# Moving the attention's subtractions and additions from GpSimd to VectorE

## The chip, the core and the metric

The kernel runs on one NeuronCore of a Trainium2 chip. The core has TensorE (PE in the profile), which multiplies matrices and writes to the accumulators in PSUM; VectorE (DVE), ScalarE (ACT) and GpSimd (POOL), which work element by element; and queues that issue transfers. Each engine runs its instructions in the order in which the program issued them to it. The metric is the device time of one execution in microseconds (us), lower is better.

## The reference

Two transformer blocks over a sequence of 1024 tokens of 1024 channels, all in float32. The change touches only the attention of the second block, which has two branches:

```python
def mla_attention(q_nope, q_rope, k_nope, k_rope, v):     # 8 heads, 64 + 32 channels for q and k, 64 for v
    ...
    logits = (einsum(qn, k_nope) + einsum(qr, k_rope)) * B_QK_DIM ** -0.5
    logits = where(causal, logits, NEG_INF)
    return einsum(softmax(logits), v)

def dsa_sparse_attention(q, k, v, iq, ik, iw, positions, rel_table):   # 8 heads, one k and v for all of them
    ...
    _, sel = top_k(score, 256)                            # per query, over the keys up to it
    logits = einsum(q, k[sel]) * A_HEAD_DIM ** -0.5 + bias
    return einsum(softmax(logits), v[sel])
```

Behind it `merged = gate_a * (y_a @ w_branch_a) + gate_b * (y_b @ w_branch_b)`, an output product with a residual, and an MLP.

## The kernel before

To keep float32 accuracy every matrix operand is held as two parts, a high half `hi` (the value rounded as ScalarE writes it) and a low half `lo = raw - hi`; a product is then three matmuls (`mm3`: hi hi, hi lo, lo hi). So nearly every operand needs a copy by ScalarE (the high half) and a subtraction behind it (the low half).

The attention (`attention`) is 16 heads one after the other, first the 8 MLA heads, then the 8 sparse (DSA) heads; a head runs over pairs of 128-row query blocks in the order 3, 0, 2, 1. `front` computes the scores into PSUM (tile `pd`, two buffers), a row maximum on VectorE, and the exponential on ScalarE. `back` transposes the probabilities on TensorE into PSUM (tile `ps`, four buffers), copies the high half (ScalarE) and subtracts for the low half (VectorE, tile `t`), multiplies with the values and scales the output.

Nothing there is issued at once. Every piece is a step of a `Plan`: an engine, an estimated duration, a rank (a wished-for time), the function that issues the instruction, the steps that it needs, and the buffers that it takes and frees. `Plan.run` plays the engines forward with the estimates and always issues what can start first; among steps of an engine that can start within 0.05 us the lowest rank goes first. This writes the order of every engine's queue. Engines named in the steps are `PE`, `ACT`, `DVE` and `Pool`. A transfer (`transfer`) is a step of 1.06 us on `Pool`, which issues it, followed by an estimated landing time. Buffers that the steps take are `pd` (2), `ps` (4), `t2` (8, of 512 columns) and `t4` (2, of 1024 columns).

The steps that the change touches make inputs of the heads and of the stage behind:

- `mla_begin`, line 2684: low half of the rotated keys, in three copies (32 rows of 1024), rank -20 and up.
- `q_rope`, line 2717: the sum of the two rotated terms of the rope queries, 512 columns, four times. Behind it `rope_rows` loads 32 rows for each MLA head (line 2787), copies the high half and subtracts (line 2798).
- `dsa_begin`, line 2904: low half of the sparse branch's keys (64 rows of 1024); `dsa_inputs`, line 2854: the same for the queries of each sparse head, behind a transfer into a `t4` buffer.
- `y_done`, line 2621: low half of y_a after each pair of sparse heads but the last (128 rows of 1024); the last pair's is on VectorE already (line 2623).
- `yb_part`, line 2934: low half of y_b, which was stored to memory and is loaded into `t2` buffers, eight times 512 columns.
- `branch_weights`, line 2472: low half of the first three weight tiles of the branch products (128 rows of 1024). Its engine is the weight stream's `lo_engine`, which line 2459 sets to GpSimd for the time of the plan and line 2465 sets back.

GpSimd's queue also issues the transfers named above. Ahead of the attention, at the end of `z_phase`, nine further weight tiles are split with GpSimd's help (line 2367 sets `lo_engine`); line 2407 sets it to VectorE before the attention starts.

## Time and profile before

| | us |
|---|---|
| median of three timed runs | 2674.82 |
| lowest and highest of them | 2673.29, 2676.94 |
| the profiled execution | 2677.41 |
| its span, first to last instruction | 2675.6 |

The profile is one execution. Its views used here: the page (busy time of each engine over the span), busy time by stretch, groups of instructions, waits (who waited for whom) and the timeline of an engine. Durations of single instructions overlap a little with the next one, so the time that an instruction takes from its engine is read between two starts. All instructions carry line 183, a recording helper, so the groups are told apart by their tiles: `t` are the `t2` and `t4` buffers, `u` the large operand buffers, `ps` and `pd` the accumulators, `wr`, `wh` and `wl` a weight tile as loaded and its two halves, `topk` the buffer that also holds the statistics of the softmax.

### The profile page before, as it was taken

What the parts mean: (1) busy time and instruction counts of PE and PEld (TensorE: products, weight loads), DVE (VectorE), ACT (ScalarE), POOL (GpSimd) and SP (SyncE); (2) the same over time, 40 slices, a digit from 0 to 9 for tenths busy, and PEclk for the clock granted to TensorE, in tenths of its full rate; (3) what the DMA queues carried; (4) which work ended last, traced back from release to release, by engine and by line L of the source; (5) the groups of instructions that cost most, each with busy time, mean ns of one, the idle gap of its engine ahead of it and who ended that gap; (6) DMA issues with size and microseconds to landing.
All of it is one profiled execution on the core that took longest, in us unless ns stands there. A gap on an engine that the chain in (4) does not pass through costs nothing.

```text
span 2675.6 us, 33677 instructions
## 1 busy us (share of the span) xinstructions
PE 2588.6 (97%) x12052; PEld 2079.3 (78%) x12052; DVE 1895.2 (71%) x3239; ACT 1334.5 (50%) x2208; POOL 366.4 (14%) x393
## 2 busy tenths in 40 slices
PE   4999999999999999999999999999999999999998
PEld 4777777777888878777878778777887888887886
DVE  6684576887665466877889878887557566646668
ACT  4562114565444343445676477885135554443334
POOL 5141111100000021000211411420000000002111
PEclk8999999999999999999999999999999999999999
DMA  6536638655445597645545501444455564459784
GB/s 207 186 106 217 192 116 272 220 185 152 147 138 197 188 268 212 190 116 170 138 150 169 185 15 40 145 149 136 149 171 160 185 224 142 154 186 268 189 252 146
DMA packets 371735, 456.98 MB, mean 171 GB/s; under 512 B 34014, under 2 KB 262285, under 8 KB 371053
## 3 DMA queue, kind: packets, MB, share of 16 engines
q1 hardware_dynamic: 332096, 311.07, 37.2%
q0 software_dynamic: 39136, 143.60, 18.8%
q8 instruction: 95, 1.56, 0.2%
q14 instruction: 76, 0.61, 0.1%
q10 hardware_dynamic: 332, 0.14, 0.0%
HBM read 361.70 MB, written 96.18 MB: 171 GB/s over the span
## 4 chain that ended last, share of the span: by engine, by line
PE 73%; DVE 10%; issue 6%; DMA 5%; ACT 4%; POOL 1%; SPq 0%; POOLq 0%; ACTq 0%; DVEq 0%
PE ps L183 50%; PE pd L183 22%; DVE u L183 4%; DVE t L183 3%; ACT u L183 2%; DMA t<-in_w_in 2%; ACT t L183 1%; DVE wl L183 1%; DVE tiny L183 1%; POOL u L183 1%; DMA slabd<-t 1%; DVE topk L183 1%; DMA u<-opd 1%; ACT wh L183 1%; DMA t<-aqd 0%
## 5 line engine op out<-in xcount | busy, mean ns | idle before, releaser
L183 PE MATMUL ps<-u,wh 128*128 128x512 f32 x3696 | 1173.3, 398 | 6.7 <-ACT u L183 4.2
L183 PEld LDWEIGHTS ps<-u,wh 128*128 128x128 f32 x3696 | 690.0, 188 | 177.0 <-ACT u L183 5.7
L183 PE MATMUL ps<-u,wl 128*128 128x512 f32 x1848 | 731.9, 396 | 0.6 <-DVE wl L183 0.6
L183 PE MATMUL pd<-u,wh 128*128 128x512 f32 x1472 | 480.3, 407 | 2.5 <-ACT u L183 1.6
L183 PEld LDWEIGHTS ps<-u,wl 128*128 128x128 f32 x1848 | 347.5, 188 | 86.4 <-DVE wl L183 1.3
L183 DVE TENSOR_TENSOR wl<-wr,wh 128x1024 fp32r<-128x1024 f32 (+3 forms) x213 | 229.9, 1080 | 162.5 <-ACT wh L183 156.0
L183 PEld LDWEIGHTS pd<-u,wh 128*128 128x128 f32 x1472 | 274.1, 190 | 70.9 <-issue 5.7
L183 PE MATMUL pd<-u,wl 128*128 128x512 f32 x736 | 292.4, 397 | 0.0
L183 ACT ACTIVATE wh<-wr 128x1024 fp32r<-128x1024 f32 (+3 forms) x225 | 207.2, 921 | 168.3 <-PE pd L183 78.9
L183 ACT ACTIVATE t<-ps 128x512 f32<-128x512 f32 (+7 forms) x347 | 176.6, 523 | 177.0 <-PE ps L183 164.1
L183 DVE TENSOR_TENSOR t<-ps,t 128x384 fp32r<-128x384 f32 (+3 forms) x354 | 192.5, 563 | 90.6 <-PE ps L183 59.7
L183 ACT ACTIVATE t<-t 128x512 f32<-128x512 f32 (+2 forms) x261 | 162.8, 626 | 168.9 <-DVE t L183 90.5
L183 DVE TENSOR_TENSOR u<-u 128x1024 fp32r<-128x1024 f32 (+3 forms) x154 | 154.1, 1002 | 68.1 <-ACT u L183 62.6
L183 ACT ACTIVATE u<-t 128x512 fp32r<-128x512 f32 (+4 forms) x158 | 127.5, 815 | 136.7 <-DVE t L183 110.8
L183 ACT ACTIVATE wh<-u 128x1024 fp32r<-128x1024 f32 x96 | 101.3, 1055 | 182.8 <-PE ps L183 116.8
L183 DVE TENSOR_TENSOR wl<-u,wh 128x1024 fp32r<-128x1024 f32 x96 | 117.3, 1222 | 88.0 <-ACT wh L183 87.9
L183 PE MATMUL ps<-wh,u 128*128 128x512 f32 (+1 forms) x576 | 173.7, 383 | 0.6 <-DVE u L183 0.6
L183 POOL DMA_DIRECT2D u<-opd x64 | 55.2, 1027 | 862.8 <-DMA u<-opd 758.2
L183 PEld LDWEIGHTS pd<-u,wl 128*128 128x128 f32 x736 | 139.2, 189 | 34.0
L183 PE MATMUL pd<-wh,u 128*128 128x512 f32 x512 | 162.0, 396 | 0.0
L183 ACT ACTIVATE u<-u 128x1024 fp32r<-128x1024 f32 (+8 forms) x111 | 97.6, 889 | 126.1 <-issue 57.1
L183 ACT ACTIVATE u<-ps 128x512 f32<-128x512 f32 (+2 forms) x171 | 95.9, 575 | 115.2 <-PE ps L183 109.2
(191 smaller groups left out, 3507.6 us busy)
## 6 DMA issues: line engine op xcount, KB each, us to landing
wr<-in_w_fc SPq DMA_DIRECT2D x64, 512.0 KB, 4.5
opd<-t SPq DMA_DIRECT2D x128, 256.0 KB, 3.7
u<-opd POOLq DMA_DIRECT2D x64, 512.0 KB, 10.5
wr<-in_w_ff SPq DMA_DIRECT2D x64, 512.0 KB, 4.5
wr<-in_w_in SPq DMA_DIRECT2D x60, 512.0 KB, 3.9
t<-opd SPq DMA_DIRECT2D x48, 512.0 KB, 4.8
u<-in_w_ada POOLq DMA_DIRECT2D x32, 512.0 KB, 4.7
wr<-in_w_out SPq DMA_DIRECT2D x32, 512.0 KB, 3.9
```

What stands on the lines that cost most here:

```text
L183: return fn(*args, **kw)
```

## The change

Each of the steps above that computes on `Pool` names `DVE` instead, with an estimate of 1.14 us (1024 columns) or 0.6 us (512 columns) in place of 2.4 and 1.3, and issues its instruction on `nc.vector`. The line that set the weight stream's engine to GpSimd for the plan is taken out. The transfers keep their engine. Nothing else is changed; the arithmetic is the same.

```diff
--- before.py
+++ after.py
@@ -2456,7 +2456,6 @@
                 t0, t1 = (clock(x + 15 * P) + self.LAG for x in (c0, c))
                 self.back(t0, n, p, (t1 - t0) / (p + 1), marks)
         ws = self.ws
-        ws.lo_engine = self.nc.gpsimd
         self.branch_weights(starts[15])
         ws.loads_ahead()
         ws.paused = True
@@ -2469,7 +2468,7 @@
         ws, step = self.ws, self.plan.step
         for i in range(3):
             a = step("ACT", 0.95, t + i, lambda i=i: ws.split_ahead(ws.used + i + 1), [self.room])
-            step("Pool", 2.4, t + i, lambda i=i: ws.parts[ws.used + i][2](), [a])
+            step("DVE", 1.14, t + i, lambda i=i: ws.parts[ws.used + i][2](), [a])
 
     def p_block(self, qb):
         p, n = qb // 2, P * (qb + 1)
@@ -2618,7 +2617,7 @@
             engine.tensor_sub(self.ya[1][:, s], x["ys"], self.ya[0][:, s].bitcast(F32))
         a = step("ACT", 0.95, t, high, needs + [self.room])
         if n < 15:
-            step("Pool", 2.4, t, lambda: low(nc.gpsimd), [a], frees=("t4",))
+            step("DVE", 1.14, t, lambda: low(nc.vector), [a], frees=("t4",))
         else:
             step("DVE", 1.2, t, lambda: low(nc.vector), [a], frees=("t4",))
 
@@ -2682,7 +2681,7 @@
             kh, kl = self.slot(i)[2:4]
             a = self.plan.step("ACT", 0.95, -20 + i, lambda kh=kh: nc.scalar.activation(kh[64:96], kr, AF.Copy))
             self.kr_steps.append(self.plan.step(
-                "Pool", 2.4, -20 + i, lambda kh=kh, kl=kl: nc.gpsimd.tensor_sub(kl[64:96], kr, kh[64:96].bitcast(F32)),
+                "DVE", 1.14, -20 + i, lambda kh=kh, kl=kl: nc.vector.tensor_sub(kl[64:96], kr, kh[64:96].bitcast(F32)),
                 [a]))
         self.qr_steps = {g: [self.q_rope(g, H) for H in range(2)] for g in range(2)}
 
@@ -2714,7 +2713,7 @@
         a = step("DVE", 0.61, rank, side, [a], takes=("t2",), frees=("ps",))
         b = step("PE", 1.3, rank, lambda: product(512), takes=("ps",))
         b = step("DVE", 0.61, rank, main, [b], frees=("ps",))
-        return step("Pool", 1.3, rank, lambda: nc.gpsimd.tensor_add(dst[:, c], dst[:, c], x["t"]), [a, b],
+        return step("DVE", 0.6, rank, lambda: nc.vector.tensor_add(dst[:, c], dst[:, c], x["t"]), [a, b],
                     frees=("t2",))
 
     def mla_inputs(self, n):
@@ -2791,11 +2790,11 @@
 
         def low():
             qh, ql = self.slot(h)[0:2]
-            nc.gpsimd.tensor_sub(ql[64:96], x["raw"][64:96], qh[64:96].bitcast(F32))
+            nc.vector.tensor_sub(ql[64:96], x["raw"][64:96], qh[64:96].bitcast(F32))
 
         a = self.transfer(2.6, t, load, self.qr_steps[h // 4] + done, takes=("t4",))
         b = step("ACT", 0.95, t + 2, high, [a])
-        return step("Pool", 2.4, t + 2, low, [b], frees=("t4",))
+        return step("DVE", 1.14, t + 2, low, [b], frees=("t4",))
 
     def latent_values(self, t, pair, c, done):
 
@@ -2845,13 +2844,13 @@
             nc.scalar.activation(self.aqs[0:64, s], x["raw"][0:64], AF.Copy)
 
         def low():
-            nc.gpsimd.tensor_sub(self.aqs[64:128, s], x["raw"][0:64], self.aqs[0:64, s].bitcast(F32))
+            nc.vector.tensor_sub(self.aqs[64:128, s], x["raw"][0:64], self.aqs[0:64, s].bitcast(F32))
 
         t = starts[8 + h] - (20 if h < 2 else 12)
         a = self.transfer(3.2, t, load, self.qk_steps.get(8 + h - 4 if h >= 4 else 7 - 2 + (h > 1), [])
                  + [self.dsa_room], takes=("t4",))
         b = step("ACT", 0.95, t + 3, high, [a])
-        c = step("Pool", 2.4, t + 3, low, [b], frees=("t4",))
+        c = step("DVE", 1.14, t + 3, low, [b], frees=("t4",))
         self.inputs[8 + h] = [c] + self.key_steps
         self.values[8 + h] = self.key_steps
         if h >= 2 and h < 6:
@@ -2878,7 +2877,7 @@
             nc.scalar.activation(self.ak[64 * i:64 * i + 64, 0:D], x["raw"][0:64], AF.Copy)
 
         def low():
-            nc.gpsimd.tensor_sub(self.ak[0:64, D:2 * D], x["raw"][0:64], self.ak[0:64, 0:D].bitcast(F32))
+            nc.vector.tensor_sub(self.ak[0:64, D:2 * D], x["raw"][0:64], self.ak[0:64, 0:D].bitcast(F32))
 
         def low_again():
             nc.scalar.activation(self.ak[64:128, D:2 * D], self.ak[0:64, D:2 * D].bitcast(F32), AF.Copy)
@@ -2902,7 +2901,7 @@
         self.dsa_room = step(None, 0.0, t, rooms, used)
         a = self.transfer(4.0, t, load, [self.dsa_room], takes=("t4",))
         b = [step("ACT", 0.95, t + 3, lambda i=i: high(i), [a]) for i in range(2)]
-        c = step("Pool", 2.4, t + 3, low, [b[0]])
+        c = step("DVE", 1.14, t + 3, low, [b[0]])
         c = step("ACT", 0.95, t + 5, low_again, [c])
         d = step("PE", 0.6, t + 4, turn, [a], takes=("ps",))
         e = step("ACT", 0.49, t + 4, v_high, [d])
@@ -2928,10 +2927,10 @@
             nc.scalar.activation(self.yb[0][:, s], x["r"], AF.Copy)
 
         def low():
-            nc.gpsimd.tensor_sub(self.yb[1][:, s], x["r"], self.yb[0][:, s].bitcast(F32))
+            nc.vector.tensor_sub(self.yb[1][:, s], x["r"], self.yb[0][:, s].bitcast(F32))
         a = self.transfer(3.2, t, load, [self.room, self.yd_steps[m]], takes=("t2",))
         b = step("ACT", 0.52, t, high, [a])
-        step("Pool", 1.3, t, low, [b], frees=("t2",))
+        step("DVE", 0.6, t, low, [b], frees=("t2",))
 
     def bias_next(self, h, qb):
         self.bias_issue(3)
```

## Rows read from the trace of the kernel before

**Rows 1.** The page: span, and busy us of each engine (share of the span).

```profile
span 2675.6 us, 33677 instructions
PE 2588.6 (97%) x12052; PEld 2079.3 (78%) x12052; DVE 1895.2 (71%) x3239; ACT 1334.5 (50%) x2208; POOL 366.4 (14%) x393
```

**Rows 2.** Busy time by stretch: start:end, length, each engine's busy us, clock, DMA.

```profile
1526.00:1640.00 114.00, 105.35 (x693) 89.61 (x693) 89.18 (x188) 82.94 (x179) 23.06 (x18) 0.96 0.11 35
1640.00:1700.00 60.00, 56.75 (x414) 48.87 (x414) 48.73 (x111) 46.58 (x102) 12.93 (x11) 1.00 0.12 35
1700.00:1770.00 70.00, 65.26 (x468) 52.68 (x467) 58.37 (x166) 62.30 (x134) 36.74 (x30) 1.00 0.63 190
1770.00:1838.00 68.00, 65.41 (x479) 53.24 (x477) 58.56 (x167) 52.85 (x124) 8.65 (x7) 1.00 0.57 175
1750.00:1760.00 10.00, 9.94 (x75) 8.07 (x74) 9.52 (x27) 8.96 (x20) 3.08 (x3) 1.00 0.55 157
```

**Rows 3.** Timeline of PE: start, us, instruction; the first product of the branches.

```profile
1845.45 0.68 PE L183 MATMUL ps<-u,wh 128*128 128x512 f32 x2
```

**Rows 4.** Waits of PE, 1506 to 1838: total us, times, longest.

```profile
PE ps L183 <- DVE t L183: 9.7, 23, 1.0
PE pd L183 <- ACT u L183: 3.1, 4, 1.1
PE ps L183 <- DVE u L183: 2.0, 5, 0.5
...
PE pd L183 <- POOL u L183: 0.5, 1, 0.5
```

**Rows 5.** Waits of DVE, 1506 to 1838.

```profile
DVE t L183 <- ACT t L183: 22.9, 46, 1.5
...
DVE t L183 <- POOL u L183: 2.1, 1, 2.1
```

**Rows 6.** Groups of POOL, 1506 to 1838: count, busy us, mean ns, idle before.

```profile
L183 POOL TENSOR_TENSOR u<-t,u 64x1024 fp32r<-64x1024 f32 x9 | 21.4, 2380 | 58.1 <-ACT u L183 57.5 <-DVE t L183 0.5
L183 POOL TENSOR_TENSOR u<-t,u 32x1024 fp32r<-32x1024 f32 x8 | 18.9, 2367 | 75.7 <-ACT u L183 75.7
L183 POOL TENSOR_TENSOR u<-t,u 128x512 fp32r<-128x512 f32 x8 | 10.1, 1281 | 3.8 <-ACT u L183 2.9 <-issue 0.8
L183 POOL TENSOR_TENSOR u<-u 32x1024 fp32r<-32x1024 f32 x3 | 7.8, 2613 | 4.3 <-issue 4.3
L183 POOL TENSOR_TENSOR u<-t,u 128x1024 fp32r<-128x1024 f32 x3 | 7.2, 2405 | 51.0 <-ACT u L183 51.0
L183 POOL TENSOR_TENSOR wl<-wr,wh 128x1024 fp32r<-128x1024 f32 x3 | 7.2, 2394 | 0.1
L183 POOL TENSOR_TENSOR u<-u,t 128x512 f32<-128x512 f32 x4 | 5.0, 1271 | 0.1
```

**Rows 7.** Timeline of DVE at the attention's start.

```profile
1506.33 1.22 DVE L183 TENSOR_TENSOR wl<-wr,wh 128x1024 fp32r<-128x1024 f32 x1
...
1507.47 0.69 DVE L183 SCALAR_TENSOR_TENSOR t<-ps,u 128x512 f32<-128x512 f32 x1
...
1508.07 0.68 DVE L183 SCALAR_TENSOR_TENSOR u<-ps,u 128x512 f32<-128x512 f32 x1
...
1509.56 0.69 DVE L183 SCALAR_TENSOR_TENSOR u<-ps,u 128x512 f32<-128x512 f32 x1 [0.22 <-PE ps L183]
```

**Rows 8.** Timeline of POOL: transfer of the rope rows, first subtractions behind it.

```profile
1517.43 1.16 POOL L183 DMA_DIRECT2D t<-u  x2 [0.30 <-POOL u L183]
1523.68 4.76 POOL L183 TENSOR_TENSOR u<-t,u 32x1024 fp32r<-32x1024 f32 x2 [5.10 <-ACT u L183]
```

**Rows 9.** Timeline of PE: one of three like waits for DVE.

```profile
1593.91 0.79 PE L183 MATMUL ps<-t,u 128*64 128x256 f32 x3 [1.04 <-DVE t L183]
```

**Rows 10.** Timeline of DVE ahead of the attention, beside a POOL subtraction.

```profile
1268.18 2.68 DVE L183 TENSOR_TENSOR u<-u,t 32x512 f32<-32x512 f32 x1
```

**Rows 11.** Waits of ACT, 1506 to 1838.

```profile
ACT u L183 <- DMA t<-u: 2.6, 1, 2.6
```

## The prediction

> **What bounds the kernel now.** I read the page's busy shares first [rows 1]: TensorE (PE) is busy 97% of the span, VectorE (DVE) 71%, GpSimd (POOL) 14%. Over the whole span PE is the bound and DVE looks half free, but that is an average over stages, and the change lies in one stage only, the attention. So the second view is the busy time by stretch [rows 2]. The attention runs from about 1506 us to 1845.45, where PE starts the branch products [rows 3]. I cut it at 1526 (first scores), 1640 and 1700 (the last latent-attention (MLA) heads give way to the sparse (DSA) heads) and 1770. The reader is to see three things in it. PE is busy 92 to 96% in every stretch, so what delays PE here moves the end one for one: the stages behind are matmuls in fixed order. DVE is busy 78, 81, 83 and 86% from 1526 on, so it is the second most loaded engine everywhere but in 1700 to 1770, where ScalarE (ACT) passes it. And POOL's work is not spread evenly: 36.7 us of it lie in those 70 us.
>
> Third, the waits of PE in the attention [rows 4]: 9.7 us for DVE's low halves of the transposed probabilities (tile t), 2.0 us for DVE's low halves of the heads' inputs (tile u), 3.1 us for ACT, and only 0.5 us for POOL. DVE itself waits once for POOL, 2.1 us, and 22.9 us for ACT's copies in 46 small pieces [rows 5]. So POOL's slow arithmetic costs almost nothing today, while DVE is already the engine that PE waits for.
>
> **The change, part by part.** It removes 38 tensor operations from POOL in seven groups [rows 6], 34 subtractions and 4 sums: 9 + 8 + 3 + 3 + 3 = 26 of 1024 columns at 2.37 to 2.61 us, and 8 + 4 = 12 of 512 columns at 1.27 to 1.28 us, together 21.4 + 18.9 + 10.1 + 7.8 + 7.2 + 7.2 + 5.0 = 77.6 us of POOL. The groups are the low halves of the sparse heads' queries and keys (64 partitions), of the rope rows (32 partitions), of y_b, of the three copies of the rope keys, of y_a and of the branch weights, and the four sums of q_rope. The transfers stay on POOL's queue.
>
> What one costs on DVE: the same operation on two operands in SBUF, 1024 columns, is shown at the border of the attention: it starts at 1506.33 and the next instruction starts at 1507.47, so it takes 1.14 us of the engine; two 512-column operations start 0.60 us apart [rows 7]. On POOL the durations follow the columns, not the partitions [rows 6]; I take the same for DVE. Added to DVE: 26 x 1.14 + 12 x 0.60 = 36.8 us. No new kind of wait arises: each subtraction still waits for ACT's high half. But it now does so in DVE's queue, in order, and behind it stand the maxima, the low halves for PE and the scaled outputs.
>
> The order of all engines is written by the planner from estimated durations, and it changes with them. I price it by stretch.
>
> *Start, to 1526: 7 of the 38* (three rope keys, two sums, two rope rows). Now POOL makes keys and sums one after the other, its transfer of the rope rows starts at 1517.43 and the first rope subtraction at 1523.68 [rows 8]; PE waits for the result 0.5 us [rows 4]. On DVE the chain is: three keys from 1507.47 [rows 7], 3.4 us, then four scalings and two sums, 6 x 0.60 = 3.6 us, so the transfer starts near 1514.8, 2.6 us earlier, and the subtraction behind it takes 1.3 us less: scores may start some 4 us earlier, and products that PE now does ahead of them are left to fill the waits behind them. Against this stand the same three keys: they rank first, so DVE frees the first PSUM buffer 3.4 us later, at 1511.5 instead of 1508.1. PE wants it when its fourth product is done, for which DVE waits until 1509.56 [rows 7]: 2 us lost, as all four buffers are then full. Bounds: -3.6 us (POOL's 0.5 and all 3.1 us of ACT's waits gone) to +3.4 us (the keys in full). They nearly cancel, I take 0.
>
> *1526 to 1700: two sums, six rope rows, four of the sparse subtractions*, 10 x 1.14 + 2 x 0.60 = 12.6 us, into 24.8 + 11.3 = 36 us of idle DVE [rows 2]. Most are wanted a head later and find room. But three rope rows (issued on POOL at 1546, 1591 and 1637) come 2 to 3 us ahead of places where PE already waits about 1 us for DVE; one of the three like places is shown [rows 9]. I take 3 x 0.8 = 2.4 us there and nothing for the rest; bounds 0 and 12.6.
>
> *1700 to 1838: five sparse subtractions, three of y_a, three branch weights, eight of y_b*, 11 x 1.14 + 8 x 0.60 = 17.3 us, of which 15.1 us fall in 1700 to 1770. DVE's 58.4 busy us become 73.5 in a stretch of 70 [rows 2]: it doesn't fit. A dense stretch of the trace has DVE busy 9.52 of 10 us with PE still at 9.94 [rows 2]; at that density 73.5 us need 77.2, +7. The y_b halves and branch weights (8.2 us) have no reader before 1845, and 1770 to 1838 has 9.4 us idle of which 2.3 are taken by y_a; so about 3 us can slide there. That leaves +4 us. Bounds: -2.1 (DVE's one wait for POOL goes [rows 5], all else hidden) and +17.3 (all on the path).
>
> Two rules of the Trainium skill bear on this. The row first: DVE at 83 to 86% [rows 2] with PE waiting for it [rows 4]. "Perfetto Trace Analysis", section Optimizing Scalar/DVE Operations, says that a saturated DVE may gain from giving work to GPSIMD; that speaks against this change, and by it the sum would be on the slow side, as mine is. The other row: ahead of the attention a 512-column DVE sum with both inputs in SBUF, 0.6 us by the price above, took 2.68 us beside a POOL subtraction [rows 10]. "SBUF — State Buffer", section Who interferes with whom, gives the reason: such an operation and a GpSimd operation that reads SBUF exclude each other. In the attention DVE reads PSUM for one operand, and the page excludes the block there; by the rule a moved subtraction costs its bare 1.14 us, as no POOL arithmetic is left beside it, and otherwise up to 2.68, 2.4 times the sum.
>
> Sum: 0 + 2.4 + 4 = +6.4 us. The profiled execution took 2677.41 us, its span 2675.6 [rows 1] and 1.8 around it; the median of the three timed runs is 2674.82, 2.6 less. I add the sum to the median: 2681.
>
> **Rivals.** *Hidden (not slower).* The planner knows DVE's price and puts the subtractions into DVE's idle 57 us (1526 to 1838). For it: the 10 us at 95% without loss [rows 2]. Against it: the 70 us with 73.5 us of work. It decides if y_b and the branch weights slide past 1770. Time: 0 + 0 to 1, 2675.
>
> *Faster.* The start chain shortens and buffers that POOL held come free. TensorE's granted clock averaged 0.96 in 1526 to 1640 [rows 2], parts of it at the lower level (1.2 GHz) after PE had idled; if the first heads start without gaps some of 0.04 x 114 = 4.6 us comes back. Price: 3 of the 3.6 at the start, 2.1 of POOL's wait, 1 of the clock, -6: 2669. Against it: the PSUM buffer held 3.4 us longer.
>
> *Stuck queue (slower by more).* Planned transfers land in 2.6 to 4.0 us, but ACT already waits for them, 2.6 us at once for a rope row [rows 11]. On POOL such a delay stopped nobody; on DVE it stops the maxima and low halves. It decides if DVE's waits ahead of moved subtractions exceed some 2 us in sum. Price: 6.4, the 3 us that then can't slide, and up to 4 us of landings: +13, 2688.
>
> That the subtractions would stay on GpSimd I leave out: each has its engine written out, and the branch weights take the stream's default, VectorE.
>
> **How the numbers follow.** 0.2% is 5.3 us, about what a measurement of this kernel can tell from no change: the bounds are 2669.5 and 2680.2. Forecast (2677.5 to 2687) 0.48: 0.32 slower, 0.16 same. Hidden 0.25: 0.24 same, 0.01 faster. Faster 0.13: 0.09 faster, 0.04 same. Stuck 0.14: slower. Together faster 0.10, same 0.44, slower 0.46. The range 2671 to 2689 takes in all of the forecast and the hidden case and half of each of the outer ones. The wide bounds of the stretches would all have to fall on one side to leave it.
>
> **What the changed profile would show.** POOL has only transfers in the attention and DVE about 36.8 us more. Start: the rope transfer near 1515, a PE wait of about 2 us at 1510, scores some 4 us earlier. DSA heads: DVE at 95% or more, PE's waits for DVE's t up from 9.7 to about 15 us, the branches' start later than 1845 by the sum. Wrong would be: DVE idle for the landing of a transfer (stuck), or y_b's subtractions far behind their ACT copies without loss for PE (hidden), or the branches starting before 1845 (faster).

## The result and the profile after

The kernel after takes 2700.74 us (median of four runs, 2698.35 to 2704.19) against 2675.88 us (2673.29 to 2680.07) for the kernel before beside it: 1.0091 times as long, 95% interval 1.0079 to 1.0104, so 25 us slower. The forecast was 2681 us, 6.4 us slower, with a range up to 2689. The sign of the likeliest case was right and the size was wrong by a factor of four. The profiled execution took 2704.19 us.

The page of after, as [rows 1]:

```profile
span 2702.4 us, 33653 instructions
PE 2602.5 (96%) x12052; PEld 2089.8 (77%) x12052; DVE 1931.6 (71%) x3277; ACT 1334.6 (49%) x2208; POOL 288.6 (11%) x355
```

VectorE has 38 instructions and 36.4 us more, GpSimd 38 instructions and 77.8 us less. These are the 36.8 and 77.6 us of the prediction. The groups on VectorE (count, busy us, mean ns, idle time before) give the price that had been read between two starts [rows 7]; 32, 64 or 128 partitions cost the same:

```profile
L183 DVE TENSOR_TENSOR u<-t,u 64x1024 fp32r<-64x1024 f32 x9 | 11.0, 1219 | 0.7 <-ACT u L183 0.3
L183 DVE TENSOR_TENSOR u<-t,u 32x1024 fp32r<-32x1024 f32 x8 | 9.7, 1217 | 1.4 <-ACT u L183 1.3
L183 DVE TENSOR_TENSOR u<-t,u 128x512 fp32r<-128x512 f32 x8 | 5.4, 682 | 1.2 <-ACT u L183 1.2
L183 DVE TENSOR_TENSOR u<-t,u 128x1024 fp32r<-128x1024 f32 x3 | 3.7, 1225 | 0.8 <-ACT u L183 0.8
```

All of the loss is in the attention. Its end, the first product of the branches, moved from 1845.45 [rows 3] to

```profile
1872.64 0.68 PE L183 MATMUL ps<-u,wh 128*128 128x512 f32 x2
```

Busy time by stretch, as [rows 2] (start:end, length, busy us of PE, PEld, DVE, ACT and POOL, clock, DMA share, GB/s), first four stretches and then the whole attention:

```profile
1526.00:1640.00 114.00, 105.12 (x683) 88.84 (x683) 95.10 (x195) 78.48 (x171) 3.60 (x7) 0.96 0.07 24
1640.00:1700.00 60.00, 52.42 (x326) 44.34 (x325) 45.85 (x93) 40.76 (x87) 2.67 (x5) 0.89 0.16 51
1700.00:1770.00 70.00, 59.26 (x405) 47.84 (x403) 61.80 (x146) 52.52 (x113) 6.91 (x13) 0.95 0.47 137
1770.00:1838.00 68.00, 64.02 (x461) 52.22 (x460) 62.06 (x167) 52.66 (x120) 0.51 (x1) 1.00 0.47 134
...
1506.00:1872.00 366.00, 330.48 (x2193) 273.95 (x2191) 311.66 (x701) 261.31 (x565) 17.34 (x33) 0.95 0.32 97
```

The reader is to see two things in 1640 to 1770. VectorE is busy 76 and 88% there, *not* 95% or more: it is idle 14 us in the first of these stretches while TensorE is idle 7.6. And the granted clock is 0.89 and 0.95, where [rows 2] have 1.00 in both.

The loss can be counted in two terms. From VectorE's last instruction ahead of the attention to the first branch product it is 339.1 us before and 366.8 after. TensorE is idle 20.9 us in it before, 35.7 after: +14.8. The trace's record of the clock has TensorE at its lower level (1.2 GHz) for 10.2 us before and 34.1 after. There the transposes of the probabilities start 0.21 us apart (128 columns each), at the higher level 0.11, so about half of that time is lost: (34.1 - 10.2) / 2 = +11.9. Together 26.7 of 27.7 us. TensorE is idle in 2.1 of the 34.1 us, which the first term has already; without them the second is 10.9. These are single executions. The mean clocks of all runs give a little less: what the span is short of full clock, (1 - clock) x span, is 39 us in after and 28 to 31 in the sets of runs of before, so 8 to 11 us. A third to nearly half of the loss is the clock.

Waits of PE and of DVE, 1506 to 1870, as [rows 4, 5] (total us, times, longest):

```profile
PE ps L183 <- DVE t L183: 17.1, 21, 4.4
PE pd L183 <- ACT u L183: 8.1, 15, 1.4
PE ps L183 <- DVE u L183: 5.5, 7, 1.2
...
DVE t L183 <- ACT t L183: 22.6, 46, 1.2
DVE u L183 <- ACT u L183: 14.2, 22, 2.4
DVE topk L183 <- PE pd L183: 6.2, 6, 2.2
```

PE's three largest waits have all grown: for DVE's `t` by 7.4, for `u` by 3.5, for ACT's `u` by 5.0. Those for POOL are gone.

**Where it lies.** I take as a head's start VectorE's first row maximum of it. Head 6 starts at 1659.5 before and 1662.6 after, head 9 at 1713.8 and 1739.5. So 3.1 us are lost up to head 6, 22.5 in heads 6 to 8 (54.3 us before, 76.8 after), and 1.6 in the seven heads behind. Heads 6 to 8 by busy time (columns as above), in before:

```profile
1659.50:1713.80 54.30, 50.91 (x371) 42.77 (x370) 44.90 (x107) 44.62 (x96) 17.37 (x15) 1.00 0.27 78
```

in after:

```profile
1662.60:1739.50 76.90, 63.67 (x404) 52.26 (x402) 60.66 (x127) 53.76 (x109) 7.08 (x14) 0.89 0.27 83
```

PE is idle 13.2 us against 3.4 there, and half of 16.5 us at the lower level is 8.2. Together that is 18 of the 22.5 us; the rest is work of TensorE that the new order has moved into these heads from others. The longest stall is at y_b. POOL issues its transfers:

```profile
1729.90 2.67 POOL L183 DMA_DIRECT2D t<-yd  x5
```

PE waits:

```profile
1733.32 0.39 PE L183 MATMUL ps<-t,u 128*128 128x256 f32 x1 [1.84 <-ACT t L183]
1738.12 0.90 PE L183 MATMUL ps<-t,u 128*64 128x256 f32 x3 [4.41 <-DVE t L183]
```

And this is what VectorE runs meanwhile:

```profile
1729.84 1.23 DVE L183 TENSOR_TENSOR wl<-wr,wh 128x1024 fp32r<-128x1024 f32 x1 [0.53 <-ACT wh L183]
1731.10 1.22 DVE L183 TENSOR_TENSOR u<-t,u 64x1024 fp32r<-64x1024 f32 x1
1732.35 2.36 DVE L183 TENSOR_TENSOR wl<-wr,wh 128x1024 fp32r<-128x1024 f32 x2
1735.16 0.69 DVE L183 TENSOR_TENSOR u<-t,u 128x512 fp32r<-128x512 f32 x1 [0.46 <-ACT u L183]
1736.58 0.69 DVE L183 TENSOR_TENSOR u<-t,u 128x512 fp32r<-128x512 f32 x1 [0.72 <-ACT u L183]
1737.37 0.69 DVE L183 TENSOR_TENSOR t<-ps,t 128x512 fp32r<-128x512 f32 x1
```

Five transfers of y_b take five of the eight `t2` buffers at once. For 7.5 us VectorE then runs moved work only: three branch weights, a sparse query, two halves of y_b, and waits for ScalarE's copies of y_b, which wait for landings. The low half that TensorE wants (`t<-ps,t`) stands seventh. On GpSimd the same work stood in nobody's way: all of PE's waits for POOL were 0.5 us [rows 4].

The clock follows such stalls. Five stretches of 3.4 us of after (same columns as above):

```profile
1670.20:1673.60 3.40, 2.31 (x15) 1.92 (x16) 3.00 (x8) 3.33 (x7) 0.00 (x0) 0.72 0.00 0
1673.60:1677.00 3.40, 3.40 (x19) 3.13 (x18) 1.33 (x3) 1.77 (x5) 0.53 (x1) 0.50 0.25 76
1731.40:1734.80 3.40, 0.47 (x2) 0.19 (x1) 3.28 (x3) 3.12 (x6) 1.18 (x3) 1.00 0.85 228
1734.80:1738.20 3.40, 0.08 (x1) 0.08 (x2) 2.21 (x4) 2.22 (x4) 0.54 (x1) 0.76 0.70 255
1738.20:1741.60 3.40, 3.40 (x16) 2.91 (x17) 3.02 (x6) 1.90 (x4) 1.12 (x3) 0.50 0.28 96
```

After the long stall the clock is 0.50 in 1738.2 to 1741.6, while TensorE is busy all of the time: the stall has been paid already, and the matmuls behind it run at half speed on top. After 1.1 us of idling within 1670.2 to 1673.6 the same is seen in the stretch behind.

### The profile page after: what moved, and what is told of

The parts are those of the page before. It is cut to its first block, busy times and chain, and to the rows that moved or that the text cites. A ratio compares the mean times of both kernels' runs of the same rounds, so it can differ in the third digit from the quotient of the medians.

```text
span 2702.4 us, 33653 instructions
## 1 busy us (share of the span) xinstructions
PE 2602.5 (96%) x12052; PEld 2089.8 (77%) x12052; DVE 1931.6 (71%) x3277; ACT 1334.6 (49%) x2208; POOL 288.6 (11%) x355
## 4 chain that ended last, share of the span: by engine, by line
PE 74%; DVE 11%; ACT 5%; issue 5%; DMA 4%; POOL 0%; SPq 0%; ACTq 0%; DVEq 0%; POOLq 0%
PE ps L183 49%; PE pd L183 25%; DVE u L183 5%; ACT u L183 3%; DVE t L183 3%; ACT t L183 1%; DMA t<-in_w_in 1%; DVE wl L183 1%; DVE tiny L183 1%; DVE topk L183 1%; ACT wh L183 1%; DMA t<-xT 1%; DMA u<-opd 1%; DMA slabd<-t 0%; DMA t<-opd 0%
## 5 line engine op out<-in xcount | busy, mean ns | idle before, releaser
L183 DVE TENSOR_TENSOR u<-u 128x1024 fp32r<-128x1024 f32 (+4 forms) x157 | 158.1, 1009 | 68.3 <-ACT u L183 65.1
L183 DVE TENSOR_TENSOR u<-t,u 128x512 fp32r<-128x512 f32 (+4 forms) x157 | 144.0, 921 | 31.8 <-ACT u L183 30.5
```

What stands on the lines that cost most here:

```text
L183: return fn(*args, **kw)
```

## The experiments

Each ratio is to runs of the kernel before beside it on the same chip. "Attention" is from VectorE's last instruction ahead of it to the first branch product in the profiled execution; "lower level" is the time at 1.2 GHz within it. All times in us. The profiled execution isn't always a typical one: in after, e1, e15, e17 and e22 it is the slowest of its runs, in e4, e20 and e21 the fastest.

| kernel | median | ratio, 95% interval | attention | PE idle | lower level |
|---|---|---|---|---|---|
| before | 2675.88 | 1 | 339.1 | 20.9 | 10.2 |
| after | 2700.74 | 1.0091 [1.0079, 1.0104] | 366.8 | 35.7 | 34.1 |
| e1_order | 2702.10 | 1.0093 [1.0077, 1.0110] | 364.6 | 41.0 | 30.7 |
| e2_engine | 2702.68 | 1.0101 [1.0085, 1.0118] | 363.5 | 34.6 | 27.3 |
| e19_few_after | 2688.17 | 1.0034 [1.0021, 1.0046] | 349.4 | 28.0 | 17.1 |
| e20_few_before | 2677.69 | 1.0000 [0.9991, 1.0010] | 338.3 | 22.5 | 3.4 |
| e4_start_rope | 2683.60 | 1.0028 [1.0015, 1.0041] | 343.3 | 23.6 | 13.7 |
| e5_dsa | 2692.46 | 1.0052 [1.0034, 1.0069] | 354.4 | 29.7 | 17.1 |
| e6_late | 2684.93 | 1.0032 [1.0016, 1.0049] | 345.2 | 25.7 | 6.8 |
| e3_no_late | 2700.51 | 1.0099 [1.0073, 1.0125] | 362.3 | 34.7 | 20.5 |
| e8_urgent_t4 | 2705.34 | 1.0102 [1.0083, 1.0121] | 363.5 | 37.8 | 27.3 |
| e12_hold | 2685.20 | 1.0030 [1.0019, 1.0041] | 346.9 | 29.3 | 17.1 |
| e13_begin_after | 2693.51 | 1.0059 [1.0041, 1.0078] | 355.1 | 32.2 | 10.2 |
| e14_begin_before | 2673.75 | 0.9983 [0.9974, 0.9993] | 336.7 | 19.4 | 13.7 |
| e15_begin_dsa | 2690.16 | 1.0044 [1.0027, 1.0060] | 351.6 | 26.8 | 20.5 |
| e16_begin_yb_after | 2687.55 | 1.0044 [1.0029, 1.0058] | 349.8 | 29.6 | 10.2 |
| e17_race_before | 2676.36 | 0.9995 [0.9985, 1.0005] | 339.5 | 20.1 | 13.7 |
| e18_begin_sums | 2676.65 | 1.0000 [0.9990, 1.0009] | 339.2 | 21.5 | 13.7 |
| e21_race_more | 2683.87 | 1.0031 [1.0019, 1.0042] | 344.8 | 26.7 | 13.7 |
| e22_begin_yb_before | 2673.74 | 0.9981 [0.9971, 0.9990] | 336.4 | 17.8 | 13.7 |

**The load on VectorE, or the order that the planner writes?** The change does both: it puts work on VectorE, and by naming `DVE` with other estimates it makes the planner write another order of all queues. e1 takes the order without the work, e2 the work without the order.

```diff
# e1: before.py, all seven kinds of step, so that only the planner sees VectorE
-        return step("Pool", 2.4, t + 2, low, [b], frees=("t4",))
+        return step("DVE", 1.14, t + 2, low, [b], frees=("t4",))     # low still issues on nc.gpsimd
# e2: before.py, so that only the instruction moves
-            nc.gpsimd.tensor_sub(ql[64:96], x["raw"][64:96], qh[64:96].bitcast(F32))
+            nc.vector.tensor_sub(ql[64:96], x["raw"][64:96], qh[64:96].bitcast(F32))   # step still "Pool", 2.4
```

> The planner is told of the change (VectorE, 1.14 and 0.6 us), so that every queue gets the order that the changed kernel has, but the 38 operations are still issued to GpSimd. Theory 'work' (VectorE's 36.8 us and what waits behind them in its queue cost the 25 us): VectorE carries nothing more, PE's stalls from 1506 us on fall from 36 back to about 21, time near 2676 to 2682. Theory 'order' (the new order of the copies, transfers and products is what costs): 2695 to 2705, with the long stall of PE near 1735 still there.

> The reverse: the planner still believes in GpSimd (2.4 and 1.3 us), so that the order is that of the kernel before, but the 38 operations are issued to VectorE at the places that this order gives. Theory 'work': near 2700, as the 36.8 us are in VectorE's queue all the same; it may be worse than the changed kernel, as the planner doesn't know of them. Theory 'order': 2676 to 2682.

Both took as long as after, so they do not separate the two. Each has a fault of its own: in e1 a result comes 1.2 us later than the planner counted on, in e2 VectorE is busy where it counted on idle time. e19 and e20 mend that. They keep the two orders and put only a small part of each operation on VectorE.

```diff
# e19: after.py, 35 of the 38 operations (not the branch weights); e20: the same cut on e2
+    def fill(self, _, out):                       # issued with ScalarE's copy
+        self.nc.gpsimd.memset(out.bitcast(F32), 0.0)
+    def few(self, out, a, b, add=0):
+        f = self.nc.vector.tensor_add if add else self.nc.vector.tensor_sub
+        f(out[:, ::16], a[:, ::16], b[:, ::16])
```

> The kernel after with its order of all engines, but 35 of the 38 operations do only every 16th column (64 or 32 of them) on VectorE, so that nearly all of the added load is gone while the planner still counts it in full; the rest of each low half is filled with zeros by GpSimd beside ScalarE's copy, and the rest of each q_rope sum is left out. The three branch weights stay whole. If the added load on VectorE makes the loss, this takes 2672 to 2684 us. If the order that the planner writes makes it, 2692 to 2701 us.

> The same cut on e2: the order of the kernel before, 35 of the operations on VectorE but on every 16th column only, zeros filled in by GpSimd, the three branch weights whole. Both theories expect 2670 to 2679 us, since neither the load nor the new order is there; a longer time would be the price of the filling.

e20 is as fast as before: in this order the filling costs nothing, and little load loses nothing. e19 lies between its two expectations. Both causes are real. With the order of before the load makes the step from e20 to e2, 1.0000 to 1.0101. With the order of after it makes the step from e19 to after, 1.0034 to 1.0091, some 15 us of 25; the other 9 us come with the order, from e20 to e19. Little load is not none: on the page VectorE is busy 10.7 us more in e19 than in before and 8.3 us more in e20, and the three branch weights are whole in both. The whole attention by busy time (columns as above), e2:

```profile
1506.00:1871.00 365.00, 330.39 (x2188) 273.75 (x2202) 313.95 (x705) 264.21 (x567) 17.53 (x33) 0.96 0.32 100
```

e19:

```profile
1506.00:1857.00 351.00, 322.97 (x2187) 269.62 (x2203) 288.05 (x705) 263.31 (x566) 40.88 (x62) 0.98 0.34 103
```

e20:

```profile
1506.00:1842.00 336.00, 313.56 (x2171) 260.88 (x2184) 283.35 (x700) 259.07 (x563) 40.34 (x61) 0.99 0.34 105
```

By the pages VectorE is busy 27.7 us more in e2 than in e20, where the attention is 25.2 us longer, and 25.7 more in after than in e19 (17.4 longer). By the table the load's step is PE idle +12.1 and (27.3 - 3.4) / 2 = 12.0 of clock in the first pair, 7.7 and 8.5 in the second. So in these executions it is half stalls and half clock; by the mean clocks of all runs the clock's part is 12 us in the first pair and 4 in the second.

The two causes don't lie in the same place. The attention of these profiles in three parts, in us:

| kernel | up to head 6 | heads 6 to 8 | heads 9 to 15 |
|---|---|---|---|
| before | 153.2 | 54.3 | 131.6 |
| e20_few_before | 149.5 | 54.3 | 134.4 |
| e2_engine | 165.8 | 57.6 | 140.0 |
| e19_few_after | 148.8 | 70.6 | 130.0 |
| after | 156.8 | 76.8 | 133.2 |

In heads 6 to 8 the order takes 16.2 us (e20 to e19) and the load only 6.3 (e19 to after), 3.3 in the old order (e20 to e2). e1, the new order with nothing on VectorE but with its fault, takes 79.2 there. The same heads by busy time in e19:

```profile
1656.40:1727.00 70.60, 59.52 (x402) 48.76 (x402) 53.75 (x127) 53.81 (x109) 14.06 (x23) 0.95 0.30 90
```

In these executions the load costs most up to head 6, 8.0 and 16.3 us, where the order costs nothing. The clock is in these numbers: e13 and e16 below, with the same operations moved, come to head 6 in 152.1 and 152.2 us, with 3.4 us at the lower level there where after has 13.6.

**One part alone.** Each of e4 to e6 is before.py with some hunks of the change taken over, estimates included; e3 is after.py without those of e6.

```diff
# e4: hunks of mla_begin, q_rope, rope_rows (15 operations)    e5: dsa_inputs, dsa_begin (9)
# e6: branch_weights, yb_part (11)                             e3: all but branch_weights, yb_part (27)
```

> Only the rope keys, the sums of q_rope and the rope rows on VectorE (15 operations of the MLA half, 14.9 us), the rest on GpSimd. In the changed kernel the heads 0 to 5 lag by 3.1 us and the heads 6 to 8 add 22.6. Theory 'local' (each stretch pays for its own operations): 2678 to 2680. Theory 'early shift' (the first heads' new order sets off what is lost later): above 2690.

> Only the sparse heads' keys and queries on VectorE (9 operations, 10.3 us), the rest on GpSimd. Theory 'load': 10.3 of 36.8 us of a loss of 25, near 2683. Theory 'held buffers': their subtractions end 1.2 to 4.8 us behind the copies in the changed kernel against 2.5 before, so alone they hold nothing longer: 2676 to 2680. If these nine are what costs 17 us between the kernel with start and rope rows alone and the one without the late parts: 2690 or more.

> Only the low halves of y_b and of three branch weights on VectorE (11 operations, 8.2 us). Theory 'load': +5 to 6, 2681. If the block of 1730 to 1738 (PE idle 6.2 us) belongs to these operations alone: +6 to +9 with half-speed clock behind it, 2683 to 2686. If they find room, as taking them out of the change moved the time by nothing: 2676.

> The change without its last two parts: the low halves of y_b and of the three branch weights stay on GpSimd (11 of the 38 operations, 8.2 us of VectorE). If the block at 1730 to 1738 (PE idle 1.84 and 4.41 us) comes from these being queued on VectorE ahead of the probabilities' low halves, PE loses some 6 us less and some of the half-speed clock behind it goes: 2690 to 2693. If the loss is VectorE's load as such, in proportion, 8.2 of 36.8 us: 2695. If these parts don't matter: 2700.

Each part alone costs: 0.28, 0.52 and 0.32%, or 7.5, 14 and 8.6 us, for 14.0, 10.9 and 7.1 us that they add to VectorE's busy time on the page. By the planner's estimates they add 14.9, 10.3 and 8.2. The sum, 30 us, is even more than the whole change (and the three operations of y_a are in none of them), so the prices don't simply add. One reason is a price that the whole change doesn't have: where GpSimd keeps some of the arithmetic, single moved operations last longer beside it. In e5 one sparse subtraction took 2.53 us, 1.22 elsewhere, and PE waited behind it:

```profile
1760.66 2.35 POOL L183 TENSOR_TENSOR u<-t,u 128x1024 fp32r<-128x1024 f32 x1 [14.64 <-ACT u L183]
1761.56 2.53 DVE L183 TENSOR_TENSOR u<-t,u 64x1024 fp32r<-64x1024 f32 x1 [1.83 <-ACT u L183]
1764.87 0.60 PE L183 MATMUL ps<-t,u 128*64 128x256 f32 x3 [2.28 <-DVE t L183]
```

In e6 two halves of y_b took 2.38 and 1.36 us instead of 0.68. That is 1.3 us of VectorE in e5 and 2.4 in e6, a part of their prices. e3 shows the same from the other side: without y_b and the branch weights nothing is won. In e5 nine operations cost more than they last, so more than their own time is lost there; heads 6 to 8 take 62.9 us. e5 and e6 came out as the last and the second case of their expectations have it, e3 as if its parts didn't matter; e4 lies between its two.

**A buffer held too long?** In after three rope subtractions stand 6.8 to 12.9 us behind their copies on VectorE (2.4 before on GpSimd), and each holds one of two `t4` buffers; the keys' transfer starts at 1653.06 instead of 1640.41. e8 gives the subtractions that free `t4` the first rank. e12 holds the buffers longer with nothing on VectorE.

```diff
# e8: after.py, the four steps of this kind             # e12: before.py
-        return step("DVE", 1.14, t + 2, low, ...)      -        nc.gpsimd.tensor_sub(ql[64:96], ...)
+        return step("DVE", 1.14, -100, low, ...)       +        for _ in range(4): nc.gpsimd.tensor_sub(ql[64:96], ...)
                                                        -    return step("Pool", 2.4, t + 2, low, ...)
                                                        +    return step("Pool", 9.6, t + 2, low, ...)
```

> The changed kernel, all 38 operations on VectorE, but the subtractions that end the use of a t4 buffer (rope rows, sparse keys and queries, y_a: 20 of them) get the lowest rank, so that VectorE takes them as soon as ScalarE's copy is there. In the changed kernel the rope rows of the heads 3, 5 and 7 end 12.9, 6.8 and 6.8 us behind their copy (2.4 before) and the transfers behind them start later (the sparse keys at 1653 instead of 1640). Theory 'held buffers' (the two t4 buffers pass all transfers of head inputs; held longer, the later heads' inputs come late, PE stalls and its clock falls): the keys' transfer returns to about 1642 and most of the 25 us go, 2680 to 2688. Theory 'load' (36.8 us more of work on a nearly full VectorE): unchanged, 2696 to 2702.

> The kernel before, nothing on VectorE, but GpSimd makes each of the eight rope subtractions four times over (9.6 us instead of 2.4, and the planner knows it), so that the t4 buffer and the transfers behind it wait 7.2 us longer. Theory 'held buffers': the same loss as in the changed kernel without any load on VectorE, +8 to +20, 2684 to 2696, with the sparse keys' transfer later than 1640. Theory 'load': 2676 to 2678.

Both speak against it. In e8 the delays fall to 1.3 to 3.2 us, the keys' transfer comes 139.6 us behind the attention's start (147.3 in after, 134.1 in before), and nothing is won. e12's time lies in the range given for held buffers, but not for that reason: its loss is one stall of 8.56 us for the first rope row, at 1536.23, whose subtraction lasts 7.2 us longer, and the clock behind it. Its keys' transfer starts at 1665.5, and heads 6 to 8 take 4.3 us more than in before, the heads behind 4.2 less.

**A buffer taken by the wrong one?** In after two loads of sparse queries go ahead of the store of y_b that ends a pair of MLA heads; in before it is one. POOL's timeline, 1664 to 1692, in before:

```profile
1665.40 0.55 POOL L183 DMA_DIRECT2D t<-aqd  x1 [3.39 <-issue]
1673.51 0.57 POOL L183 DMA_DIRECT2D yd<-t  x1 [0.54 <-DVE t L183]
```

in after:

```profile
1674.54 0.53 POOL L183 DMA_DIRECT2D t<-aqd  x1 [20.92 <-PE ps L183]
1684.14 0.51 POOL L183 DMA_DIRECT2D t<-aqd  x1 [9.07 <-DVE u L183]
1685.51 0.56 POOL L183 DMA_DIRECT2D yd<-t  x1 [0.85 <-DVE topk L183]
```

in e13:

```profile
1680.02 0.54 POOL L183 DMA_DIRECT2D yd<-t  x1 [30.21 <-DVE t L183]
1683.19 0.53 POOL L183 DMA_DIRECT2D t<-aqd  x1 [2.63 <-DMA yd<-t]
```

A load that nobody needs yet then has the `t4` buffer that the running pair's output tile wants. e13 makes each such load wait until that tile has its buffer; e14 does it to before, e15 to e5.

```diff
+        if new:                                              # back(): first step of a pair's output tile
+            self.begins = {**getattr(self, "begins", {}), n // 2: first}
-                 + [self.dsa_room], takes=("t4",))           # dsa_inputs(): the load
+                 + [self.dsa_room, self.begins[(8 + h) // 2 - 1]], takes=("t4",))
```

> The changed kernel, all 38 operations on VectorE, and one more condition for the planner: the load of a sparse head's queries into a t4 buffer waits until the output tile ys of the pair of heads before has taken its own t4 buffer. Theory 'buffer race' (with VectorE's quicker subtraction a t4 buffer comes free about a microsecond earlier, before the running pair's output is asked for, and a load that isn't urgent takes it; the outputs of that pair, and the probability buffers behind them, then wait for another round): the heads 6 to 8 lose 10 us or more less, 2684 to 2692. Theory 'load': unchanged within 3 us, 2698 to 2704.

> The same condition in the kernel before. Theory 'buffer race': the race is there too, though it is mostly won by the output tile; PE's work moves earlier by a few us, 2670 to 2676. Theory 'load': 2676, no change.

> The same condition in the kernel that has only the nine subtractions of the sparse keys and queries on VectorE, which took 2692.5. Theory 'buffer race': 2676 to 2682, nearly the whole 15 us, as the work of nine subtractions (10.3 us) finds room in VectorE's idle time. Theory 'load': 2688 to 2694.

e13 wins 0.32 of the 0.91% back, and the time at the lower level is that of before; the whole is 1.5 us above the range of its first theory. Heads 6 to 8 take 60.7 us, 16 less than in after, and head 9 starts 5.7 us later than in before, not 25.7. But head 9, where y_b now lies, takes 25.1 us instead of 20.3, with the moved halves ahead of a row maximum:

```profile
1731.06 0.73 PE L183 MATMUL pd<-u 128*128 128x512 f32 x2 [2.17 <-DVE topk L183]
```

e14 is faster than both kernels, 0.9983 of before. e15 missed its expectation: heads 6 to 8 take 53.6 us, as in before, and other places lose instead (head 0 at the start, heads 9 to 13). Its head 9 takes 25.4 us with y_b's halves on GpSimd, so the moved halves are not the only way to that length; in e15 one sparse subtraction there lasts 4.02 us beside GpSimd's work, and PE waits 3.21 us behind it. e17 and e21 then lose that buffer with nothing moved to VectorE, by a wait of the tile for the load:

```diff
# e21: before.py
+        if h == 1:                                           # dsa_inputs(): head 9's load
+            issue, begin = a.needs[0], self.begins[3]        # output tile of head 6's pair
+            begin.needs.append(issue); issue.users.append(begin); begin.wait += 1
# e17: and the loads behind it stay behind the tile
-                 + [self.dsa_room], takes=("t4",))
+                 + [self.dsa_room] + ([self.begins[3]] if h in (2, 3) else []), takes=("t4",))
```

> Nothing is moved to VectorE. In the kernel before, the output tile of head 6's pair is made to wait until head 9's load of queries has been issued, so that it gets its buffer of t4 late, as it did in the kernel after. If the lost buffer alone costs heads 6 to 8 their time, they take some 62 to 75 us instead of 54.3 and the whole some 2684 to 2697 us. If the lost buffer costs only together with the load on VectorE (or if the rest of the changed order is what cost), heads 6 to 8 stay within 2 us of 54.3 and the whole within 2674 to 2679 us.

> e17 without its second condition, so that further loads of queries may go ahead of the output tile of head 6's pair too. In e17 that tile began only 5.4 us later than before (counted from the start of the attention, 173.3 us against 167.9), in after 17.1 us later (185.0); here it should be later by 10 us or more, still with nothing on VectorE. If a tile that late costs by itself, heads 6 to 8 take 65 us or more instead of 54.3 and the whole 2682 to 2697 us. If it costs only with the rest of the change, the whole stays within 2674 to 2680 us.

PE's first instruction on that tile comes 167.9 us after the attention's start in before, 185.0 in after, 168.4 in e13, 173.3 in e17 and 170.4 in e21. e17's 5 us are absorbed: heads 6 to 8 take 57.1 us, 2.8 more than before where 2 were allowed, and the whole is unchanged. In e21 the instruction is no later, against the expectation of 10 us, but PE then stands for a step behind it:

```profile
1684.43 1.63 PE L183 MATMUL ps<-t,u 128*128 128x256 f32 x4 [7.73 <-ACT t L183]
```

ScalarE in these microseconds:

```profile
1675.63 1.06 ACT L183 ACTIVATE u<-t 64x1024 fp32r<-64x1024 f32 x1 [2.26 <-DMA t<-aqd]
1677.50 1.06 ACT L183 ACTIVATE u<-t 64x1024 fp32r<-64x1024 f32 x1 [0.80 <-DMA t<-aqd]
1682.84 1.06 ACT L183 ACTIVATE u<-t 64x1024 fp32r<-64x1024 f32 x1 [4.28 <-DMA t<-aqd]
1683.80 1.53 ACT L183 ACTIVATE t<-ps 128x512 fp32r<-128x512 f32 x3
```

With three query loads ahead, ScalarE stands waiting for their landings, and the copies that TensorE wants are behind it. Heads 6 to 8 take 66.0 us, the whole 1.0031. So the order of loads and output tile can cost 8 us with no work on VectorE, near the 9 of e19; but after has no such single stall there, so it is shown that this order can cost, not that it costs in the same way.

**What is left without both knots.** e16 is e13 with each load of y_b waiting for the subtraction of the one before it.

```diff
-        a = self.transfer(3.2, t, load, [self.room, self.yd_steps[m]], takes=("t2",))
+        a = self.transfer(3.2, t, load, [self.room, self.yd_steps[m]] + getattr(self, "yb_last", [])[-1:][:1], takes=("t2",))
-        step("DVE", 0.6, t, low, [b], frees=("t2",))
+        self.yb_last = getattr(self, "yb_last", []) + [step("DVE", 0.6, t, low, [b], frees=("t2",))]
```

> As the first of these, and each load of y_b waits until the subtraction of the one before is done, so that y_b holds one of the eight t2 buffers instead of five. If the remaining stall near 1730 to 1738 (1.84 and 4.41 us) comes from the t2 buffers that y_b holds: 3 to 6 us less than the first. If it comes from VectorE's work in that stretch: the same time as the first.

All 38 operations are on VectorE, and the time is 1.0044 of before's, half of the loss. It is faster than e13 by 4 us by the ratios and 6 by the medians, as expected if the stall comes from the buffers that y_b holds, but the two intervals overlap. Heads 9 to 12 of e16 (columns as above):

```profile
1719.00:1795.00 76.00, 69.37 (x470) 55.23 (x477) 73.23 (x186) 62.08 (x136) 5.99 (x11) 0.98 0.60 169
```

and nearly the same work in before:

```profile
1714.00:1785.00 71.00, 65.83 (x474) 53.42 (x473) 58.68 (x167) 60.95 (x136) 33.31 (x24) 1.00 0.59 180
```

Here VectorE is busy 96% and TensorE 91%. This is the picture that the prediction drew for 1700 to 1770, and its price, 5 us for 14.5 us more of VectorE's work, 1.5 of them by the clock (0.98 of 76 us), is near the +4 of the sum. (Against e22 below, the better control, heads 9 to 12 take 6.4 us more.) e22 is the control, the same two conditions on before:

> The kernel before with both conditions of e16 (the sparse head's query load behind the output tile, each y_b load behind the subtraction of the one before), nothing on VectorE: the control of e16. If e16's rest of 0.44% is the load's, this takes 2672 to 2678 us, as before or e14. If the conditions themselves cost, it takes more than 2680 us.

It is as fast as e14, 0.9981. So at the same conditions the load takes 1.0044 against 0.9981, some 17 us, through two sets of runs of before. In the profiles heads 6 to 8 take 60.7 us in e16 and 53.9 in e22, heads 9 to 12 75.9 and 69.5, heads 13 to 15 61.0 and 57.6. Up to head 6 e16 is 3.2 us shorter, but by the clock: PE is idle 14.6 us there against 9.8, and at the lower level for 3.4 us against 13.7. So the load costs in every stretch, not only where it doesn't fit.

**A smaller part of the change on the better order.** e18 is e14 with the four q_rope sums on VectorE, 2.7 us of work.

```diff
-        return step("Pool", 1.3, rank, lambda: nc.gpsimd.tensor_add(dst[:, c], dst[:, c], x["t"]), [a, b],
+        return step("DVE", 0.6, rank, lambda: nc.vector.tensor_add(dst[:, c], dst[:, c], x["t"]), [a, b],
```

> The kernel before with the condition of e14 (the sparse head's query load waits for the output tile of the pair before), and of the change only the q_rope sums on VectorE. If each operation on VectorE costs its time there, this is e14 plus at most 2 us (2674 to 2676). If the shorter sums let the first heads start sooner and nothing else follows, 2671 to 2673 us.

It loses e14's gain: 1.0000 against 0.9983, again through two sets of runs of before. The first two sums took 1.58 us instead of 0.68 beside GpSimd's rope keys, so a part of this is again the price of arithmetic on both engines. No part of the change was found that pays; the two conditions alone (e14, e22) are worth 0.17 to 0.19%.

## Why the prediction was right and wrong

**Right: the prices and the stall at the start.** The work added is 36.4 us for 36.8. At the start PE has the predicted stall, 2.3 us for 2:

```profile
1511.31 1.22 PE L183 MATMUL ps<-u,wh 128*128 128x512 f32 x2 [2.32 <-DVE t L183]
```

The transfer of the rope rows on POOL, which was to come at 1514.8 and had been at 1517.43 [rows 8]:

```profile
1517.07 1.15 POOL L183 DMA_DIRECT2D t<-u  x2 [15.11 <-DVE u L183]
```

So the gain of 2.6 us there was only 0.4. Scores didn't start 4 us earlier: counted from VectorE's last instruction ahead of the attention, head 0 starts 1.0 us later than in before and head 1 0.7 us later, for a sum of 0.

**Right by luck: the stretch to head 6.** The term was +2.4 and the trace has +3.1. But up to there PE is idle 5.0 us more than in before and at the lower level for 3.4 us more; it comes out at 3.1 because the new order has left some 3 us of TensorE's work for later heads. The load's price there is 3.3 us by e13 and 8.0 by after, both against e19, and 16.3 in the old order.

**Wrong: the planner's new order was named and not priced.** The prediction says that the order of all engines "changes with them" and prices "by stretch", but behind the start no term holds anything for it, and most of what was moved in 1526 to 1700 got "nothing for the rest". This is the step that failed where most was lost: after loses 22.5 us in heads 6 to 8, and 16.2 of them are there in e19, at 10.7 us of the 36.4 us of work. Over the whole the order costs 9 us, as other heads gain by it. e13 and e16 win back 8.6 and 12.6 us of after's loss by two changes of order, and e21 loses 8 us by one, without any load. In e19 itself the five-fold transfer of y_b ends in PE waits of 1.80 and 3.19 us, as in after:

```profile
1725.65 0.90 PE L183 MATMUL ps<-t,u 128*64 128x256 f32 x3 [3.19 <-DVE t L183]
```

The branch weights, which e19 does in full, are in VectorE's queue ahead of it, so this stall is not the order's alone; which decisions make the rest of the 9 us stays open.

**Wrong: the price of the load.** The sum takes VectorE's load as three waits of 0.8 us up to 1700 and as the time by which 73.5 us don't fit into 70, +4 us. It was made from 10 us of the kernel before where VectorE is busy 95% without loss [rows 2]; that density was taken for what the planner would reach anywhere. In after VectorE is idle a quarter of 1640 to 1700. It was not full; as at y_b, it ran moved work or waited for that work's input while TensorE waited for something behind it. A queue in order costs by what stands ahead of the wanted instruction, not by the sum over a stretch. Two pairs at the same order and one at the same conditions price the load: 1.01% for 27.7 us of work (e2 and e20), 0.57% for 25.7 (after and e19), 0.63% for 34.0 (e16 and e22), so 27, 15 and 17 us, 0.5 to 1 us for each us of work. The sum had 6.4 for 36.8.

**Wrong: the clock had a price in one rival only, as a gain.** The faster rival got 1 us back from it. In after it costs 11 to 12 of 27.7 us in the profile, 8 to 11 by all runs. The row that pointed to it was there: 0.96 in 1526 to 1640 [rows 2], beside a start with stalls. The added stalls of after (14.8 us) brought more than half of their own length again by the clock; a term of the sum that is a stall needed both.

**The range.** The bounds of the three stretches went up to 3.4 + 12.6 + 17.3 = 33 us, and 27 were lost, within them. The range left the upper part out since the bounds "would all have to fall on one side". They didn't have to: 3.1 us are lost up to head 6, 1.6 from head 9 on, and the rest in the three heads between. The bounds were made of the load alone, and neither the order nor the clock was in them, so it shows little that the loss lies within them.

**The rivals.** Stuck queue is partly right: the stall of 4.41 us has VectorE waiting 0.46 and 0.72 us for y_b's halves, which ScalarE makes as the transfers land. By its own condition, more than 2 us of VectorE's waits ahead of moved operations, it applies: 0.7 + 1.4 + 1.2 + 0.8 in the groups above. But in that place the weights and the query ahead of them did more. Hidden falls: work that nobody reads before the branches (y_b and the branch weights, e6) costs 8.6 us; with it heads 9 to 12 take 77.1 us instead of 71.3. Faster falls: with VectorE at 78 to 86% [rows 2], below saturation, the kernel that leaves the work on GpSimd is the faster one. The page "Perfetto Trace Analysis" of the Trainium skill (section Optimizing Scalar/DVE Operations) says that a saturated DVE may gain from giving work to GPSIMD, and that it might not help as the two share a read port; the first half pointed the right way. The price of 2.68 us beside GpSimd [rows 10] didn't appear in after, where GpSimd has no arithmetic left in the attention: no group of moved operations has a mean above 1.23 us. It did appear in e5, e6, e15 and e18, where some is left.

## What to carry to other kernels

Work that is moved to the engine for which the bound engine waits is not hidden by that engine's idle share: here it cost from half of its duration to all of it, and the slow engine that nobody waited for was the better place. Add to the stalls what the clock takes behind them: some 10 us on 14.8 here. Where a planner writes the order, time the new order without the new load and the new load in the old order (e19, e20 and e2 here) before one of them is called the cause, and give an order that is named a term or a bound of its own. A stretch that comes out as its term says can still be two errors that cancel.

## What the runs showed of the hardware

The granted clock is 0.50 in stretches where TensorE is busy without a gap, 3.40 of 3.40 us, behind stalls; in all TensorE was at the lower level for 3.4 us of the attention in e20 and for 34.1 in after. A VectorE subtraction doesn't shrink in proportion to its columns: 64 columns in steps of 16 took 0.27 us and 32 columns 0.21 (e19), against 0.68 for 512 and 1.22 for 1024. And beside arithmetic of GpSimd such an operation can last twice as long or more: 1.58 us for 0.68 (e18), 2.53 and 4.02 for 1.22 (e5, e15).
